# The first stage of a two-layer recurrent decoder step: order of its products, its sums of squares and one group's tables

## Chip, cores and metric

The kernel runs on one core of one Trainium2 chip. The metric is the device time of one execution in microseconds (us); the time before is the median of three runs.

## The reference, cut to what matters

One inference step of two layers over 1024 prompt tokens and 8 single new tokens, 1032 columns in all, model width 1024, float32. Each layer is

```
h = x * rsqrt(mean(x*x) + 1e-6) * norm_g
p = h @ w_in            # split over three groups of heads: HGRN2, GLA, S5
out = x + concat(group outputs, each gated) @ w_out
```

The third group (S5) takes two of the projections' tiles of 128 columns, called u here, and runs a diagonal complex recurrence over it. Its tables are powers of exp(A dt), so they need sines and cosines of small arrays (128 x 112). A last RMS norm follows the second layer.

## The kernel before, in words

Everything is held transposed: features on the 128 partitions, tokens along the free axis, cut into three blocks of 384, 384 and 264 columns (`BLK`). The width of 1024 is 8 slabs of 128 (`KD`). A float32 product is made of three products of rounded parts: weights and activations are each split into a high part (`wh`, `hh`) and a rest (`wl`, `lo`), and `wh*hh + wh*lo + wl*hh` is summed in PSUM over the 8 slabs (`gemm_tile`, L302). So one weight tile costs 24 products for each block. The norm's factor is applied last, when a finished sum leaves PSUM, so products can start before the norm is known.

Weights come through `WStream` (L252): halves of a tile are loaded (256 KB, two buffers), and each quarter is split by `do_split` (L274): ACT makes `wh`, then POOL or DVE makes `wl`. Six pairs of such quarters are held at a time; a tile takes four.

The first stage of layer 0 is written out by hand. `first_parts` (L220) issues the loads of x block by block with weight halves between them, and lets `parts` (L212) make `hh` on ACT and `lo` on DVE for each slab and block. Then two weight tiles (`UC0` and `UC0 + 1`, the third group's u) are multiplied (L714 to L719): the first for all blocks, the second block by block, and after each block `first_norm` (L236) squares x in place (ACT six of eight slabs, POOL two), adds the eight squares to two by six additions shared by DVE and POOL (L245), and sums these over the partitions by two products with a matrix of ones (`ones`, float32, not the rounded type). `rstd` (L200) turns the sum into the norm's factor `rn`: two operations on ACT, four on DVE. `ev_uc` (L700) multiplies the six finished sums by `rn` on DVE, which frees their six PSUM banks (two of the tag o, three of g, one of aux).

`masks()` (L1513) loads three masks; `prep(0)` starts `s5_prep` (L373), the third group's tables: some 36 small dependent DVE operations from L404 to L437, then powers by POOL (L362 to L367, tile `s5E` in `s5_thread`, L467). Both stand before the first stage's products in the text of layer 0.

The next work of TensorE in the text is a small projection `rbT` (PSUM tag o), then the projections of the second group (tag g). The order on each engine is not that of the text alone: a planner at build time lists the instructions of each engine by the order of the text and by when they become ready in its own model. Products that add to one PSUM bank keep the order of the text, and each engine's list is then fixed.

Of the kernel before, what the change touches and what calls it, by code (L numbers as in the profile page):

```python
# [38 lines left out]
def tile_hybrid_step(ctx: ExitStack, tc: tile.TileContext, a: dict, nl=NL, limit=RANGE):  # L39
# [160 lines left out]
    def rstd(pr, b):  # L200

        o, n = BLK[b]
        r = rn[:, o:o + n]
        t = tmp("sl", [P, 512], F32R).bitcast(F32)[:, :n]
        act(out=r, in_=pr, func=AF.Ln, scale=1.0 / 1024.0, bias=epsc)
        act(out=r, in_=r, func=AF.Exp, scale=-0.5)
        V.tensor_tensor(out=t, in0=r, in1=r, op=ALU.mult)
        V.scalar_tensor_tensor(out=t, in0=pr, scalar=1024.0 * EPS, in1=t, op0=ALU.add, op1=ALU.mult)
        V.tensor_scalar(out=t, in0=t, scalar1=-0.5 / 1024.0, scalar2=1.5, op0=ALU.mult, op1=ALU.add)
        V.tensor_tensor(out=r, in0=r, in1=t, op=ALU.mult)  # L210
# [9 lines left out]
    def first_parts(vec):  # L220
        xs = [alloc("x", [P, NT]) for _ in range(KD)]
        lo[:] = blocks(F32R)
        for b in range(3):
            o, n = BLK[b]
            for k in range(KD):
                if b == 0 and k % 4 == 0 or b and k == 0:
                    W.load(k // 4 if b == 0 else b + 1)
                SY.dma_start(out=xs[k][:, o:o + n], in_=a["xT"][:, k, o:o + n])
            for k in range(KD):
                if b == 0 and k % 2 == 0:  # L230
                    W.do_split(k // 2, V)
                parts(xs[k][:, o:o + n], k, b, vec)
        SY.dma_start(out=ident, in_=a["c_ident"])
        return xs

    def first_norm(xs, b):  # L236
        o, n = BLK[b]
        x = [t[:, o:o + n] for t in xs]
        for k in range(KD):
            if k % 4 == 3:  # L240
                G.tensor_tensor(out=x[k], in0=x[k], in1=x[k], op=ALU.mult)
            else:
                act(out=x[k], in_=x[k], func=AF.Square)
            if k > 1:
                (V if k % 2 else G).tensor_tensor(out=x[k % 2], in0=x[k % 2], in1=x[k], op=ALU.add)  # L245
        pr = psum("aux")
        for i in range(2):
            mm(pr[:, :n], ones, x[i], start=(i == 0), stop=(i == 1))
# [124 lines left out]
    def s5_prep(l, d):  # L373
# [30 lines left out]
        V.tensor_tensor(out=sn, in0=k14, in1=th.unsqueeze(1).to_broadcast([P, 14, 8]), op=ALU.mult)  # L404
# [255 lines left out]
    def layer(l, slow=False):  # L660
# [3 lines left out]
        wt = [W.push(a["wf"][l, i]) for i in range(25)]  # L664
# [21 lines left out]
        if l == 0:  # L686
            masks()
            prep(0)
# [22 lines left out]
        if l == 0:  # L711

            late = []
            gemm_tile(wt[UC0], [0, 1, 2], hrhs, lambda b, p: late.append(p), banks=("o", "o", "aux"))  # L714
            for b in range(3):
                gemm_tile(wt[UC0 + 1], [b], hrhs, lambda b, p: late.append(p), last=(b == 2))
                first_norm(xs, b)
                ev_uc(0)(b, late[b])
                ev_uc(1)(b, late[3 + b])  # L719
            for x in xs:  # L720
                release(x)
        else:
# [909 lines left out]
```

## Time and profile before

| | us |
|---|---|
| median of 3 runs (lowest to highest) | 1052.39 (1051.87 to 1053.72) |
| the profiled execution's own time | 1056.13 |
| its span, first to last instruction | 1054.2 |
| TensorE (PE) busy | 994.6 (94%) |
| VectorE (DVE) busy | 649.4 (62%) |
| ScalarE (ACT) busy | 479.2 (45%) |
| GpSimd (POOL) busy | 472.2 (45%) |

PE is the engine to look at: a gain elsewhere counts where it shortens a stretch in which PE waits or runs slowly. Matmuls overlap one another, so the time from the start of one to the start of the next is what one costs, not its duration.

### The profile page before, as it was taken

How to read it: one execution, taken by the hardware profiler on the slowest of the kernel's cores; microseconds unless marked ns; L12 is line 12 of the kernel's file. 1: busy time of each engine (PE TensorE's matmuls, PEld its weight loads, DVE VectorE, ACT ScalarE, POOL GpSimd, SP SyncE). 2: the span in 40 equal slices, each digit the busy share in tenths (PEclk: the TensorE clock that was granted, in tenths of full speed). 3: DMA queues.
4: the chain of work that ended last, by engine and by line, in shares of the span. 5: the costliest groups of instructions: out<-in, count | busy, mean ns of one | idle time of the engine just before them, and what ended most of it. 6: DMA issues, size and time to landing. Idle time of an engine off the chain costs nothing.

```text
span 1054.2 us, 20947 instructions
## 1 busy us (share of the span) xinstructions
PE 994.6 (94%) x8071; PEld 940.2 (89%) x8071; DVE 649.4 (62%) x1333; ACT 479.2 (45%) x995; POOL 472.2 (45%) x668
## 2 busy tenths in 40 slices
PE   6899999999999899999999999999999989999992
PEld 5788898899988799999999999888998988999991
DVE  8986745744767746685464682684388775553344
ACT  7334224554434656633332423445554475664431
POOL 4685754115355535542181476431344453552233
PEclk9999999899999989999999999999999998999996
DMA  7131131111111121144323114112111112112313
GB/s 245 46 107 51 42 107 46 59 50 56 54 40 38 57 73 60 48 137 136 128 78 92 48 41 113 45 47 61 41 56 53 41 53 70 54 48 88 116 51 135
DMA packets 78811, 76.77 MB, mean 73 GB/s; under 512 B 24524, under 2 KB 60652, under 8 KB 78700
## 3 DMA queue, kind: packets, MB, share of 16 engines
q1 hardware_dynamic: 78700, 75.33, 23.6%
q8 instruction: 65, 1.06, 0.4%
q14 instruction: 46, 0.38, 0.1%
HBM read 58.01 MB, written 15.53 MB: 70 GB/s over the span
## 4 chain that ended last, share of the span: by engine, by line
PE 68%; DVE 15%; POOL 7%; ACT 3%; issue 3%; DMA 2%; SPq 1%; DVEq 0%; POOLq 0%; ACTq 0%
PE ps_g L156 54%; PE ps_aux L156 8%; PE ps_o L156 5%; DVE s5W L584 1%; DVE Sp L897 1%; ACT ep L146 1%; DVE ep L873 1%; PE ps_aux L850 1%; POOL wl L289 1%; DVE onorm L1045 1%; DMA x<-in_xT 1%; ACT sg L146 1%; DVE wl L289 1%; DVE sl L907 1%; POOL s5E L364 1%
## 5 line engine op out<-in xcount | busy, mean ns | idle before, releaser
L156 PE MATMUL ps_g<-hh,wl 128*128 128x384 f32 (+1 forms) x1176 | 382.1, 326 | 4.5 <-POOL wl L289 4.5
L156 PE MATMUL ps_g<-hh,wh 128*128 128x384 f32 (+1 forms) x1176 | 384.6, 327 | 0.0
L156 PE MATMUL ps_g<-lo,wh 128*128 128x384 f32 (+1 forms) x1176 | 380.9, 324 | 0.0
L156 PEld LDWEIGHTS ps_g<-hh,wl 128*128 128x128 f32 x1176 | 223.5, 190 | 8.8 <-POOL wl L289 6.8
L156 PEld LDWEIGHTS ps_g<-hh,wh 128*128 128x128 f32 x1176 | 223.7, 190 | 5.3 <-issue 3.1
L156 PEld LDWEIGHTS ps_g<-lo,wh 128*128 128x128 f32 x1176 | 223.8, 190 | 1.0
L289 POOL TENSOR_TENSOR wl<-raw,wh 128x256 fp32r<-128x256 f32 x127 | 109.6, 865 | 219.9 <-ACT wh L146 207.0
L146 ACT ACTIVATE wh<-raw 128x256 fp32r<-128x256 f32 x258 | 102.2, 411 | 123.9 <-PE ps_g L156 111.5
L156 PE MATMUL ps_g<-m,wh 128*128 128x384 f32 (+1 forms) x567 | 135.7, 321 | 0.0
L289 DVE TENSOR_TENSOR wl<-raw,wh 128x256 fp32r<-128x256 f32 x131 | 82.1, 627 | 42.3 <-ACT wh L146 34.5
L156 PEld LDWEIGHTS ps_g<-m,wh 128*128 128x128 f32 x567 | 98.9, 188 | 0.5
L156 PE MATMUL ps_g<-m,wl 128*128 128x384 f32 (+1 forms) x261 | 82.9, 320 | 0.0
L1350 POOL TENSOR_TENSOR z<-z,sg 128x384 f32<-128x384 f32 (+1 forms) x48 | 47.3, 986 | 44.8 <-ACT sg L146 43.6
L156 PEld LDWEIGHTS ps_g<-m,wl 128*128 128x128 f32 x261 | 49.0, 188 | 0.1
L741 DVE TENSOR_TENSOR z<-ps_g,rn 128x384 f32<-128x384 f32 (+1 forms) x48 | 24.4, 509 | 32.8 <-PE ps_g L156 32.7
L146 ACT ACTIVATE sg<-z 128x384 f32<-128x384 f32 (+1 forms) x48 | 23.4, 487 | 28.9 <-DVE z L1348 28.7
L1360 DVE SCALAR_TENSOR_TENSOR onorm<-z,vec,onorm 128x384 f32<-128x384 f32 (+1 forms) x36 | 23.0, 639 | 21.3 <-POOL z L1350 21.2
L156 PE MATMUL ps_g<-vx,wh 128*128 128x384 f32 (+1 forms) x129 | 34.1, 322 | 0.0
L146 ACT ACTIVATE sg<-sg,ones 128x384 f32<-128x384 f32 (+2 forms) x52 | 32.3, 622 | 0.8
L146 ACT ACTIVATE sg<-sg 128x384 f32<-128x384 f32 (+2 forms) x56 | 31.8, 568 | 1.7 <-DVE sg L778 0.8
L156 PE MATMUL ps_o<-qs,Sp 64*64 64x64 f32 x360 | 23.4, 301 | 8.6 <-DVE Sp L897 8.6
L156 PEld LDWEIGHTS ps_o<-qs,Sp 64*64 64x64 f32 x360 | 21.2, 199 | 10.8 <-DVE Sp L897 9.6
(385 smaller groups left out, 1802.1 us busy)
## 6 DMA issues: line engine op xcount, KB each, us to landing
raw<-in_wf SPq DMA_DIRECT2D x100, 256.0 KB
raw<-in_wo SPq DMA_DIRECT2D x32, 256.0 KB
x<-in_xT SPq DMA_DIRECT2D x16, 192.0 KB
ext<-in_xT SPq DMA_DIRECT2D x16, 192.0 KB
x1d<-ext SPq DMA_DIRECT2D x16, 192.0 KB
ext<-x1d SPq DMA_DIRECT2D x16, 192.0 KB
usd<-ucp SPq DMA_DIRECT2D x4, 512.0 KB
s5U<-usd SPq DMA_DIRECT2D x32, 64.0 KB
```

What stands on the lines that cost most here:

```text
L146: return S.activation(out=out, in_=in_, func=func, **kw)
L156: return TE.matmul(out=out, lhsT=lhsT, rhs=rhs, start=start, stop=stop)
L289: e.tensor_tensor(out=wl, in0=r, in1=wh.bitcast(F32), op=ALU.subtract)
L364: e.tensor_tensor(out=dr, in0=dr, in1=t, op=ALU.subtract)
L584: V.tensor_tensor_scan(out=W_[:, ri, q], data0=m8[:, q0 + q:q0 + q + 1].to_broadcast([P, P]), data1=W_[:, ri, q], initial=0.0, op0=ALU.mul ...
L741: V.tensor_tensor(out=dst[:, o:o + n], in0=p, in1=rn[:, o:o + n], op=ALU.mult)
L850: TE.transpose(out=p[:, c * P:(c + 1) * P], in_=f[:, t0:t0 + P], identity=ident)
L873: V.tensor_tensor_scan(out=g[:, cs], data0=zero[:pr].to_broadcast([pr, ch]) if plus is None else plus[:, cs], data1=x[:, cs], initial=0.0, ...
L897: V.tensor_tensor_scan(out=s[:, :64 * n], data0=s[:, :64 * n], data1=kv[:, :64 * n], initial=0.0, op0=ALU.mult, op1=ALU.add)
L907: V.tensor_tensor(out=sl, in0=sq, in1=sh.bitcast(F32), op=ALU.subtract)
L1350: G.tensor_tensor(out=z[:, c], in0=z[:, c], in1=sg[:, c], op=ALU.mult)
L1360: V.scalar_tensor_tensor(out=on[:, c], in0=z[:, c], scalar=g, in1=on[:, c], op0=ALU.mult, op1=ALU.mult)
```

## The change

High parts first: for all three blocks and both tiles of u, the products with `hh` come first (`wh`, then `wl`), and the products with `lo` follow in a second pass; all six sums stay open in six PSUM banks. The second tile gets two slots of its own (`own`), so that both tiles are resident, and its loads and splits move up into the loading of x. The six additions of each block go, and eight products with ones replace two. The squares on ACT are held behind the last `hh` of the next block. `masks()` and `prep(0)` move behind the norm, and the sine and cosine chain's first operation (L404) is held behind the last `rn`. Splits made during loading alternate between DVE and POOL. `later` only orders two instructions of one engine's list.

```
@@ -207,7 +207,7 @@
         V.tensor_tensor(out=t, in0=r, in1=r, op=ALU.mult)
         V.scalar_tensor_tensor(out=t, in0=pr, scalar=1024.0 * EPS, in1=t, op0=ALU.add, op1=ALU.mult)
         V.tensor_scalar(out=t, in0=t, scalar1=-0.5 / 1024.0, scalar2=1.5, op0=ALU.mult, op1=ALU.add)
-        V.tensor_tensor(out=r, in0=r, in1=t, op=ALU.mult)
+        last["rn"] = V.tensor_tensor(out=r, in0=r, in1=t, op=ALU.mult)
 
     def parts(x, k, b, vec):
 
@@ -218,20 +218,33 @@
                                op0=ALU.mult, op1=ALU.subtract)
 
     def first_parts(vec):
+
         xs = [alloc("x", [P, NT]) for _ in range(KD)]
         lo[:] = blocks(F32R)
         for b in range(3):
             o, n = BLK[b]
             for k in range(KD):
-                if b == 0 and k % 4 == 0 or b and k == 0:
-                    W.load(k // 4 if b == 0 else b + 1)
+                if b < 2 and k % 4 == 0:
+                    W.load(2 * b + k // 4)
                 SY.dma_start(out=xs[k][:, o:o + n], in_=a["xT"][:, k, o:o + n])
             for k in range(KD):
-                if b == 0 and k % 2 == 0:
-                    W.do_split(k // 2, V)
-                parts(xs[k][:, o:o + n], k, b, vec)
+                if b < 2 and k % 2 == 0:
+                    W.do_split(4 * b + k // 2, G if k % 4 else V)
+                g = vec[:, V_NG + k:V_NG + k + 1]
+                x = xs[k][:, o:o + n]
+                h = hh[:, k, o:o + n]
+                last["hh", b] = act(out=h, in_=x, func=AF.Copy, scale=g)
+                last["lo", b] = V.scalar_tensor_tensor(out=lo[b][:, k, :], in0=x, scalar=g, in1=h.bitcast(F32), op0=ALU.mult,
+                                                       op1=ALU.subtract)
         SY.dma_start(out=ident, in_=a["c_ident"])
         return xs
+
+    last = {}
+
+    def later(i, other):
+
+        tc.add_manual_dep(getattr(i, "ins", i), getattr(other, "ins", other).name,
+                          mybir.DependencyInfo(mybir.DependencyClass.NoSync, mybir.DependencyReason.DATA), reason="order")
 
     def first_norm(xs, b):
         o, n = BLK[b]
@@ -240,12 +253,11 @@
             if k % 4 == 3:
                 G.tensor_tensor(out=x[k], in0=x[k], in1=x[k], op=ALU.mult)
             else:
-                act(out=x[k], in_=x[k], func=AF.Square)
-            if k > 1:
-                (V if k % 2 else G).tensor_tensor(out=x[k % 2], in0=x[k % 2], in1=x[k], op=ALU.add)
+                i = act(out=x[k], in_=x[k], func=AF.Square)
+                later(i, last["hh", min(b + 1, 2)])
         pr = psum("aux")
-        for i in range(2):
-            mm(pr[:, :n], ones, x[i], start=(i == 0), stop=(i == 1))
+        for k in range(KD):
+            mm(pr[:, :n], ones, x[k], start=(k == 0), stop=(k == KD - 1))
         rstd(pr[:, :n], b)
 
 
@@ -401,7 +413,9 @@
         V.tensor_tensor(out=th, in0=li, in1=dt, op=ALU.mult)
         G.tensor_tensor(out=lk, in0=k14[:, :8], in1=ld.unsqueeze(1).to_broadcast([P, 8, 8]), op=ALU.mult)
         act(out=mag, in_=lk, func=AF.Exp)
-        V.tensor_tensor(out=sn, in0=k14, in1=th.unsqueeze(1).to_broadcast([P, 14, 8]), op=ALU.mult)
+        i = V.tensor_tensor(out=sn, in0=k14, in1=th.unsqueeze(1).to_broadcast([P, 14, 8]), op=ALU.mult)
+        if l == 0:
+            later(i, last["rn"])
         V.tensor_scalar(out=n, in0=sn, scalar1=1.0 / (2 * PI), scalar2=MAGIC, op0=ALU.mult, op1=ALU.add)
         V.tensor_scalar(out=n, in0=n, scalar1=MAGIC, scalar2=None, op0=ALU.subtract)
         V.scalar_tensor_tensor(out=r, in0=n, scalar=-C1, in1=sn, op0=ALU.mult, op1=ALU.add)
@@ -661,7 +675,8 @@
         decodes[0] = 0
         vec = lv["vec"]
         col = lambda c: vec[:, c:c + 1]
-        wt = [W.push(a["wf"][l, i]) for i in range(25)]
+        own = [alloc("w1", [P, 2, 2, 2, P], F32R) for _ in range(2)] if l == 0 else []
+        wt = [W.push(a["wf"][l, i], [x[:, j] for x in own for j in range(2)] if own and i == 1 else None) for i in range(25)]
         if l == 0:
             with foreign():
                 pass
@@ -683,9 +698,6 @@
         vdd = dram.tile([8, 768], F32, name=nm("vdd"))
         st, onorm = {}, {}
 
-        if l == 0:
-            masks()
-            prep(0)
         wrr = tmp("kst", [P, 8, 16])
         SY.dma_start(out=wrr, in_=a["wr"][l])
         wr = tmp("Sp", [P, 1024], F32R)[:, :768].rearrange("p (k r c) -> p k r c", r=3, c=32)
@@ -710,15 +722,33 @@
 
         if l == 0:
 
-            late = []
-            gemm_tile(wt[UC0], [0, 1, 2], hrhs, lambda b, p: late.append(p), banks=("o", "o", "aux"))
+            late = [[psum("o"), psum("o"), psum("aux")], [psum("g") for _ in range(3)]]
+            W.do_split(9)
+            for part in range(2):
+                for b in range(3):
+                    o, n = BLK[b]
+                    for i in range(2):
+                        p = late[i][b][:, :n]
+                        ws = [W.get(wt[UC0 + i], k) for k in range(KD)]
+                        if part:
+                            for k, (wh, wl) in enumerate(ws):
+                                mm(p, wh, lo[b][:, k, :], start=False, stop=(k == KD - 1))
+                        else:
+                            for k, (wh, wl) in enumerate(ws):
+                                mm(p, wh, hh[:, k, o:o + n], start=(k == 0), stop=False)
+                            for k, (wh, wl) in enumerate(ws):
+                                mm(p, wl, hh[:, k, o:o + n], start=False, stop=False)
             for b in range(3):
-                gemm_tile(wt[UC0 + 1], [b], hrhs, lambda b, p: late.append(p), last=(b == 2))
                 first_norm(xs, b)
-                ev_uc(0)(b, late[b])
-                ev_uc(1)(b, late[3 + b])
+                for i in range(2):
+                    ev_uc(i)(b, late[i][b][:, :BLK[b][1]])
+            W.do_split(4 * wt[UC0 + 2] + 3)
+            for x in own:
+                release(x)
             for x in xs:
                 release(x)
+            masks()
+            prep(0)
         else:
             for i in range(2):
                 gemm_tile(wt[UC0 + i], [0, 1, 2], hrhs, ev_uc(i))
```

## Rows read from the trace of the kernel before

**Rows 1.** The page, part 1 (busy by engine) and part 4 (the chain by engine).
```profile
PE 994.6 (94%) x8071; PEld 940.2 (89%) x8071; DVE 649.4 (62%) x1333; ACT 479.2 (45%) x995; POOL 472.2 (45%) x668
...
PE 68%; DVE 15%; POOL 7%; ACT 3%; issue 3%; DMA 2%; SPq 1%; DVEq 0%; POOLq 0%; ACTq 0%
```

**Rows 2.** Busy us (and instructions) of each engine by stretch; then granted clock, DMA.
```profile
core 0: us, PE busy (x) PEld busy (x) DVE busy (x) ACT busy (x) POOL busy (x), PEclk, DMA share, GB/s
5.70:12.00 6.30, 5.22 (x14) 3.81 (x14) 5.36 (x16) 4.81 (x11) 1.51 (x2) 1.00 1.01 338
12.00:17.50 5.50, 3.75 (x12) 3.43 (x13) 5.50 (x12) 5.03 (x12) 3.67 (x4) 0.72 1.03 345
...
24.50:35.40 10.90, 8.90 (x51) 7.03 (x51) 10.79 (x25) 6.02 (x17) 5.18 (x7) 1.00 0.08 24
```

**Rows 3.** Timeline of PE in the first stage: start, duration, instruction, idle before and releaser.
```profile
5.71 0.69 PE L156 MATMUL ps_o<-hh,wh 128*128 128x384 f32 x1 [5.71 <-ACT hh L146]
...
14.49 0.69 PE L156 MATMUL ps_o<-lo,wh 128*128 128x384 f32 x1 [1.75 <-DVE lo L217]
...
17.54 0.48 PE L156 MATMUL ps_g<-hh,wh 128*128 128x384 f32 x1
...
22.06 0.34 PE L156 MATMUL ps_o<-lo,wh 128*128 128x384 f32 x1
...
23.11 0.34 PE L156 MATMUL ps_o<-lo,wh 128*128 128x384 f32 x1
...
30.20 0.28 PE L156 MATMUL ps_aux<-lo,wh 128*128 128x264 f32 x1
...
31.42 0.28 PE L156 MATMUL ps_g<-hh,wl 128*128 128x264 f32 x1
...
44.76 0.39 PE L156 MATMUL ps_o<-hh,Sp 128*96 128x384 f32 x1 [1.35 <-DVE s5p L430]
```

**Rows 4.** Timeline of PE: one product with ones, and the second product behind it.
```profile
39.09 0.81 PE L156 MATMUL ps_aux<-x,ones 128*128 128x384 f32 x2
...
39.91 0.34 PE L156 MATMUL ps_g<-hh,wh 128*128 128x384 f32 x1
```

**Rows 5.** Timeline of ACT while the first block of x arrives.
```profile
8.27 0.61 ACT L146 ACTIVATE hh<-x,vec 128x384 fp32r<-128x384 f32 x1 [0.97 <-DMA x<-in_xT]
...
9.20 0.70 ACT L146 ACTIVATE wh<-raw 128x256 fp32r<-128x256 f32 x2
...
11.15 1.61 ACT L146 ACTIVATE hh<-x,vec 128x384 fp32r<-128x384 f32 x3
```

**Rows 6.** Groups by line and shape, 0 to 60 us: busy, mean ns, idle before.
```profile
L217 DVE SCALAR_TENSOR_TENSOR lo<-x,vec,hh 128x384 fp32r<-128x384 f32 x16 | 11.9, 758 | 0.8 <-ACT hh L146 0.8
...
L245 POOL TENSOR_TENSOR x<-x,x 128x384 f32<-128x384 f32 x6 | 7.6, 1271 | 0.9 <-ACT x L146 0.9
```

**Rows 7.** Timelines of DVE and POOL: the tables' last steps, the powers' first and last.
```profile
46.09 0.26 DVE L433 TENSOR_TENSOR s5p<-s5p 128x112 f32<-128x112 f32 x1
...
46.23 0.41 POOL L438 COPY pv<-s5p 128x56 f32<-128x56 f32 x2 [0.92 <-DVE s5p L432]
...
70.28 0.73 POOL L367 TENSOR_TENSOR s5E<-s5E,s5Bm 128x256 f32<-128x256 f32 x1
```

**Rows 8.** Groups of the third group's output `yc`: durations min/median/max, first and last start.
```profile
L1358 DVE TENSOR_TENSOR yc<-z,yc x6: 421/546/558, 392.5 to 409.8; 128x384 f32<-128x384 f32 x4, 128x264 f32<-128x264 f32 x2
...
L785 POOL TENSOR_TENSOR yc<-yc,sg x2: 2415/2421/2427, 236.8 to 246.7; 128x1032 f32<-128x1032 f32 x2
```

**Rows 9.** Timelines of PE and DVE around the third group's product with `t`.
```profile
82.21 0.39 PE L156 MATMUL ps_aux<-ud,t 128*128 128x8 f32 x2 [1.76 <-DVE bm L879]
...
86.22 0.33 PE L156 MATMUL ps_g<-hh,wh 128*128 128x384 f32 x1
...
91.30 0.56 DVE L741 TENSOR_TENSOR vf<-ps_g,rn 128x384 f32<-128x384 f32 x1 [4.76 <-PE ps_g L156]
```

**Rows 10.** Busy us by stretch, the end of layer 0's recurrences; columns as in rows 2.
```profile
300.00:372.00 72.00, 61.99 (x740) 58.03 (x740) 49.40 (x86) 38.68 (x81) 37.02 (x40) 0.91 0.16 48
```

**Rows 11.** Waits of PE, 100 to 140 us: total us, times, longest.
```profile
PE ps_g L156 <- POOL wl L289: 1.3, 1, 1.3
```

## The prediction

> **What bounds the kernel now.** I read the page first: PE is busy 94% of the span and carries 68% of the chain that ended last [rows 1]. So the question for any edit is what it adds to PE's work and what it takes from the time in which PE waits or runs slowly. Then the stretches of the first stage: DVE is busy without a gap from 12.0 to 17.5 us and for 10.79 of the 10.90 us up to 35.4, while PE is busy only 3.75 of 5.50 us in the one and 8.90 of 10.90 in the other [rows 2]. Then PE's own timeline, for what it waits for (`lo` from DVE, as at 14.49) and at what pace it runs [rows 3]. The first stage does lose PE time, and to DVE.
>
> **How much it loses.** From the first product (5.71) to the first product behind the stage (44.76) pass 39.05 us [rows 3]. The work in it: two tiles, three blocks, 24 products each, so 96 products of 384 columns and 48 of 264. Unhindered, they cost 0.175 us (six from 22.06 to 23.11) and 0.122 us (ten from 30.20 to 31.42) [rows 3]: 96 x 0.175 + 48 x 0.122 = 22.66 us. To this come six products with ones. From 39.09 to 39.91 PE does one of them and one plain product [rows 4], so it costs 0.82 - 0.175 = 0.645 us, 3.7 times a plain one; for 264 columns 0.645 x 264/384 = 0.443. Four and two of these are 3.47 us. Lost are 39.05 - 22.66 - 3.47 = 12.92 us. That is all the stage can give back.
>
> **The change part by part.**
>
> Products with ones: eight for two in each block, so 18 more, 12 x 0.645 + 6 x 0.443 = +10.40 us of PE. Could they hide in PE's waits? The waits lie early, before the squares exist: the change holds block 0's squares behind block 1's last `hh`, and x, loaded at 338 to 345 GB/s to the end of the stretch at 17.5 [rows 2], sets when that is. I count them in full.
>
> What is still lost afterwards. (a) In one bank products keep their order, so PE first needs all eight `hh` of block 0 with `wh`, and cannot fill in `lo` and `wl` products as before. ACT has slab 3 at 8.27; slab 4 half a microsecond later, a pair of weight splits (0.70), slabs 5 to 7 (1.61) [rows 5]; without the squares that lay between them the eighth is there at about 8.27 + 0.5 + 0.5 + 0.7 + 1.61 = 11.6. PE will have done 8 x 0.175 = 1.4 us of work in 5.9: 4.5 lost. (b) From then on work is plentiful (the `wl` products of block 0, the second tile, block 1), and PE should be dense. But it enters this stretch after a sparse one. After its waits before 14.49 PE made nine products in 3.05 us (to 17.54), 1.48 us more than at full pace [rows 3], in a stretch whose granted clock is 0.72 [rows 2], that is partly at 1.2 instead of 2.4 GHz. I take 1.5 lost here too. Bounds for (b): nothing, if the clock is up by 11.6, to 1.5 plus the 2.0 us that PE idles between 24.5 and 35.4 [rows 2], if the fixed order meets late `lo` again. I take 1.5, since the entry is like that at 14.49 and DVE is relieved (below).
> On this clock the Trainium skill speaks against the change (TensorE: Matmul & The Clock Gate, Part 1: The HAM clock gate): the throttled state is the default and activity releases it. The slow products after 14.49 agree with it. By it the thin start leaves the array slow, and the sum is the one below; the granted clock of 1.00 that the row writes for 5.7 to 12.0 [rows 2], taken at its word, would make it 1.5 us less.
>
> The sum for the stage: +10.40 - 12.92 + 4.5 + 1.5 = **+3.5 us**, between +2.0 and +5.5.
>
> DVE and POOL additions: 18 go. POOL's took 1.27 us each, and `lo` beside them takes 758 ns on average [rows 6]. This is what lets `lo` come in time; its worth is already in the waits counted as gone, so it has no term of its own.
>
> Loads, splits, slots: no product or byte is added. The second tile's second half (256 KB) moves from before block 2 into the middle of block 1, whose last four slabs come 0.8 us later at 345 GB/s [rows 2], while PE is still behind with block 0. Cost nothing; were PE not behind, 0.8 us. On SP the masks' loads stand behind the norm, with each later one waiting for the cast before; queued behind them are weight halves of tiles needed only after `rbT`. Nothing, bounded by the 2.0 us of idle time above.
>
> Masks and tables: the chain of about 36 DVE operations may not start until the last `rn`, which needs PE's last product with ones, at about 44.8 + 3.5 = 48.3. Each follows the one before by some 0.2 us (0.26 long at the end of the chain [rows 7]): over 7 us, plus some 2.5 for the norm's own operations. The tables come at about 58 instead of 46.3, and the powers on POOL (46.23 to 71.0 [rows 7]) some 12 us later. Who waits? The third group's output is made by 249 us and first used at 392.5 [rows 8], 143 us of cover. So the delay itself costs nothing; what it does is to meet other work elsewhere, which the rivals price.
>
> The span would be 1054.2 + 3.5 = 1057.7. That execution took 1056.13 us itself, 3.7 above the median of the runs shown; I add the difference to the median: 1052.4 + 3.5 = **1055.9**. About 0.2% (2.1 us) can be told from no change.
>
> **The rivals.**
>
> Not slower: the wait at 82.21. PE stands 1.76 us before the third group's product with `t`, because the copy that makes `t` is queued on DVE behind the second group's scans, and PE then runs slowly until 86.22 [rows 9]. At the pace of nine products in 3.05 us, 48% of those 4.0 us are lost, 1.9; in all 3.7. With the third group 12 us later, that copy falls at about 93, where DVE waits for PE (4.76 us idle before 91.30 [rows 9]). Then 3.5 - 3.7 = -0.2: 1052.2. For it: the place is plain. Against it: PE's list is fixed at build time, and a product placed too early stalls as well at 93 as at 82. It decides once 1.4 of the 3.7 us are gone.
>
> Faster: the above, and less waiting at the end of layer 0, where PE is busy only 61.99 of 72 us [rows 10]. There the recurrences of the first group hold PE up. If the second group's get DVE and POOL before the third group's, the chain starts earlier relative to PE. A quarter of the 10 us: -0.2 - 2.5 = -2.7, so 1049.7. Against it: that chain starts from products which come 3.5 us later.
>
> Slower still: POOL. Its powers, now 12 us later, come between weight splits that PE needs; one wait of this kind is there already, 1.3 us [rows 11]. Three more: +3.9, so 1059.8.
>
> The change doing less than it says is possible in one way only: the planner may still put early `lo` products between high ones of other banks. That moves none of the terms, since PE is dense there.
>
> **How the numbers follow.** The forecast (+2.0 to +5.5, 1054.4 to 1057.9) gets 0.37: its terms are counts times measured spacings, and only the 6.0 of new losses is estimated. POOL 0.10. Not slower 0.27, as its place is clear but the list is fixed. Faster 0.26: two gains together, but each wait downstream is re-planned, and I can't exclude that more of them go than come. So slower 0.47, same 0.27, faster 0.26. The range, 1049.0 to 1060.0, leaves out about half of the faster case and a little of the POOL case, under 2 in 10.
>
> **What would show it.** In the profile after: 24 products with ones, each in two records, 0.645 us for 384 columns; the first eight products spread to about 11.6; a dense PE from there to about 48; `rn` of the last block near 51; the tables at about 58. I am wrong if PE is past the stage before 44.8 us, which needs less than 2.5 us lost in it, or if the wait at 82 is gone with nothing in its place.

## The result and the profile after

The kernel after takes 1058.84 us (median of five runs, 1057.22 to 1061.42), the kernel before 1052.39 in the same comparison: a ratio of 1.0061, with a 95% interval of 1.0043 to 1.0078, so 4.5 to 8.2 us slower. The forecast was 1055.9 in a range of 1049.0 to 1060.0. Sign and range were right. Where the time went was only half right, as the profile shows.

The profiled execution took 1058.75 us, its span is 1056.9. Of the kernel before a second execution was profiled later (the first experiment below: span 1050.3), and both are used here, because the one shown ahead of the prediction was itself 3.7 us above its median.

The page of the kernel after, parts 1 and 4, answers to [rows 1]:

```profile
PE 1002.7 (95%) x8107; PEld 947.6 (90%) x8107; DVE 653.9 (62%) x1322; ACT 477.8 (45%) x995; POOL 459.9 (44%) x661
...
PE 69%; DVE 15%; POOL 8%; ACT 4%; issue 2%; DMA 1%; SPq 0%; DVEq 0%; POOLq 0%; ACTq 0%
```

PE is busy 8.1 us more than in the execution shown ahead of the prediction, and 10.2 more than in the second (992.5); it still sets the span. So the time has to be looked for in PE's work and in PE's waits.

Busy time by stretch, columns as in [rows 2]; the first three rows answer to [rows 2], the fourth to [rows 10], the last is new and serves as a measure for every kernel below:

```profile
5.70:12.00 6.30, 4.99 (x10) 3.10 (x11) 5.61 (x11) 5.51 (x13) 2.11 (x4) 1.00 1.02 349
12.00:17.50 5.50, 5.50 (x30) 5.50 (x30) 5.50 (x9) 5.47 (x13) 3.65 (x4) 1.00 1.08 369
24.50:35.40 10.90, 10.90 (x72) 10.10 (x71) 3.95 (x12) 4.26 (x13) 3.02 (x5) 1.00 0.19 59
300.00:372.00 72.00, 68.07 (x775) 64.64 (x772) 53.23 (x107) 38.03 (x78) 40.83 (x43) 0.95 0.17 50
...
50.00:300.00 250.00, 237.59 (x1928) 218.90 (x1928) 160.78 (x341) 97.36 (x182) 119.00 (x188) 0.97 0.20 60
```

In the first stage the products run dense: from 12.0 to 17.5 us PE is busy for the whole stretch at a granted clock of 1.00 (3.75 of 5.50 us and 0.72 before), from 24.5 to 35.4 it never stops, and DVE has fallen from 10.79 to 3.95 us. DVE no longer holds PE up there. But from 50 to 300 us PE now stands idle for 250 - 237.59 = 12.41 us; in the second execution of the kernel before it is 6.19:

```profile
50.00:300.00 250.00, 243.81 (x2055) 223.97 (x2053) 154.48 (x328) 101.41 (x190) 126.48 (x183) 0.99 0.21 62
```

The timeline of PE, which answers to [rows 3, 4, 9]:

```profile
5.74 1.19 PE L156 MATMUL ps_o<-hh,wh 128*128 128x384 f32 x2 [5.74 <-ACT hh L146]
7.28 1.20 PE L156 MATMUL ps_o<-hh,wh 128*128 128x384 f32 x2 [0.34 <-ACT hh L146]
9.39 2.20 PE L156 MATMUL ps_o<-hh,wh 128*128 128x384 f32 x4 [0.92 <-ACT hh L146]
11.40 2.32 PE L156 MATMUL ps_o<-hh,wl 128*128 128x384 f32 x8
13.55 1.39 PE L156 MATMUL ps_o<-lo,wh 128*128 128x384 f32 x7
...
33.37 14.04 PE L156 MATMUL ps_aux<-x,ones 128*128 128x384 f32 x48
47.05 0.53 PE L156 MATMUL ps_o<-hh,Sp 128*96 128x384 f32 x1
...
97.84 0.45 PE L156 MATMUL ps_g<-hh,wl 128*128 128x384 f32 x1 [2.45 <-POOL wl L301]
...
105.45 0.28 PE L156 MATMUL ps_aux<-ud,t 128*128 128x8 f32 x2
```

The stage can be read off in these rows. Eight thin products until 11.40; then the products stand 0.320 us apart until 13.0 and 0.175 from 13.2 on, full pace; the 24 products with ones (48 records) in one block from 33.37; the next stage at 47.05, that is 2.3 us later than the 44.76 of [rows 3] and 3.05 later than the 44.00 of the second execution. The product with `t` no longer waits (1.76 us of wait in [rows 9]), but it has another place: 105.45 instead of 82.21. The planner has listed PE's work anew. And at 97.84 PE waits 2.45 us for a weight split from POOL, which it did not before.

DVE's timeline has the held chain, which answers to [rows 7]:

```profile
50.31 0.27 DVE L416 TENSOR_TENSOR s5p<-s5q,sm 128x112 f32<-128x112 f32 x1
50.49 0.55 DVE L839 TENSOR_TENSOR sq<-ps_o,rn 96x384 f32<-96x384 f32 x1
...
62.68 0.62 DVE L851 TENSOR_SCALAR sB<-ps_o,vec 128x384 f32<-128x384 f32 x1
63.22 0.27 DVE L442 TENSOR_TENSOR s5p<-s5p 128x112 f32<-128x112 f32 x1
...
65.52 0.55 DVE L451 TENSOR_TENSOR pw<-s5q,s5p 128x64 f32<-128x64 f32 x2
```

And POOL's the end of the tables and of the powers:

```profile
65.77 0.81 POOL L452 COPY pv<-s5p 128x56 f32<-128x56 f32 x2
...
96.38 0.72 POOL L376 TENSOR_TENSOR s5E<-s5E,s5Bm 128x256 f32<-128x256 f32 x1
97.06 0.72 POOL L301 TENSOR_TENSOR wl<-raw,wh 128x256 fp32r<-128x256 f32 x1
...
99.00 0.73 POOL L379 TENSOR_TENSOR s5E<-s5E,s5Bm 128x256 f32<-128x256 f32 x1
```

The chain starts right behind the last `rn`, at 50.31, but takes until 65.77. Its steps are 0.2 to 0.3 us long; between them DVE does the scalings of the next stage (`sq`, `sB`, `vf`), at 0.5 us and more each. So the tables come 19.5 us later than in [rows 7], not 12, and the powers end at 99.7 instead of 71.0. At 97.06 a weight split stands among them, the one PE waits for at 97.84.

The waits of PE from 75 to 300 us, which answer to [rows 11] (total us, times, longest):

```profile
PE ps_g L156 <- POOL wl L301: 3.3, 2, 2.4
PE ps_aux L1174 <- ACT s5Bm L146: 2.8, 1, 2.8
...
PE ps_aux L156 <- POOL s5O L620: 1.4, 1, 1.4
```

`s5Bm` and `s5O` are tiles of the third group. The wait for `s5Bm` is a chain of three engines: ACT's copy out of a PSUM bank into `s5Bm` waits for POOL's powers, and PE (163.15) waits for that bank with transposes of the second group. ACT's row:

```profile
162.50 0.60 ACT L146 ACTIVATE s5Bm<-ps_aux 128x512 f32<-128x512 f32 x1 [7.03 <-POOL s5E L379]
```

And the group's output, which answers to [rows 8]:

```profile
L1388 DVE TENSOR_TENSOR yc<-z,yc x6: 423/546/558, 399.5 to 416.8; 128x384 f32<-128x384 f32 x4, 128x264 f32<-128x264 f32 x2
...
L815 POOL TENSOR_TENSOR yc<-yc,sg x2: 2409/2416/2422, 254.1 to 263.9; 128x1032 f32<-128x1032 f32 x2
```

It is made at 254 to 266 and used at 399.5: 133 us of cover are left. The output was never late, and still the time was lost before it. At its first use the kernel is 10.5 us behind the second execution of the kernel before (399.5 against 389.0): 3.05 by the stage's end, 7.4 between. The span is only 6.6 longer, so 3.9 of them come back later, and no run shows where from.

### The profile page after: what moved, and what is told of

Its sections match the earlier page's. It is cut to its first block, busy times and chain, and to the rows that moved or that the text cites. A ratio compares the mean times of both kernels' runs of the same rounds, so it can differ in the third digit from the quotient of the medians.

```text
span 1056.9 us, 21006 instructions
## 1 busy us (share of the span) xinstructions
PE 1002.7 (95%) x8107; PEld 947.6 (90%) x8107; DVE 653.9 (62%) x1322; ACT 477.8 (45%) x995; POOL 459.9 (44%) x661
## 4 chain that ended last, share of the span: by engine, by line
PE 69%; DVE 15%; POOL 8%; ACT 4%; issue 2%; DMA 1%; SPq 0%; DVEq 0%; POOLq 0%; ACTq 0%
PE ps_g L156 52%; PE ps_aux L156 9%; PE ps_o L156 6%; DVE ep L903 2%; DVE s5W L598 2%; DVE Sp L927 1%; ACT ep L146 1%; DVE onorm L1075 1%; POOL s5E L376 1%; PE ps_aux L880 1%; POOL wl L301 1%; DVE qbd L954 1%; DVE wl L301 1%; POOL s5Bm L375 1%; POOL s5E L377 1%
## 5 line engine op out<-in xcount | busy, mean ns | idle before, releaser
L156 PE MATMUL ps_g<-hh,wl 128*128 128x384 f32 (+1 forms) x1152 | 374.7, 326 | 6.9 <-POOL wl L301 5.8
L156 PE MATMUL ps_g<-hh,wh 128*128 128x384 f32 (+1 forms) x1152 | 375.3, 326 | 0.0
L156 PE MATMUL ps_g<-lo,wh 128*128 128x384 f32 (+1 forms) x1152 | 373.2, 324 | 0.0
L156 PEld LDWEIGHTS ps_g<-hh,wl 128*128 128x128 f32 x1152 | 219.1, 190 | 11.9 <-POOL wl L301 7.8
L156 PEld LDWEIGHTS ps_g<-hh,wh 128*128 128x128 f32 x1152 | 219.0, 190 | 4.0 <-issue 2.0
L156 PEld LDWEIGHTS ps_g<-lo,wh 128*128 128x128 f32 x1152 | 218.6, 190 | 1.6 <-issue 0.6
L301 POOL TENSOR_TENSOR wl<-raw,wh 128x256 fp32r<-128x256 f32 x127 | 105.5, 833 | 246.5 <-ACT wh L146 226.2
L937 DVE TENSOR_TENSOR sl<-sq,sh 128x512 fp32r<-128x512 f32 x24 | 20.5, 853 | 15.3 <-ACT sh L146 15.3
```

The costliest lines, as they stand in the source:

```text
L156: return TE.matmul(out=out, lhsT=lhsT, rhs=rhs, start=start, stop=stop)
L301: e.tensor_tensor(out=wl, in0=r, in1=wh.bitcast(F32), op=ALU.subtract)
L937: V.tensor_tensor(out=sl, in0=sq, in1=sh.bitcast(F32), op=ALU.subtract)
```

## The experiments

Each kernel's ratio is to the kernel before, run beside it. "Stage's end" is the start of the first product with `Sp` on PE, "tables" the start of the copy to `pv` on POOL, "idle" is 250 us less PE's busy time between 50 and 300 us, "clock" the granted clock of that stretch, "first use" the start of the first `yc<-z,yc`, with its distance from the stage's end behind it. All but the ratio come from one profiled execution each.

| kernel | ratio, 95% interval | stage's end | tables | idle, clock | first use, distance |
|---|---|---|---|---|---|
| before, second execution | 1 | 44.00 | 45.47 | 6.19, 0.99 | 389.0, 345.0 |
| after | 1.0061, 1.0043 to 1.0078 | 47.05 | 65.77 | 12.41, 0.97 | 399.5, 352.5 |
| e1 | 0.9986, 0.9971 to 1.0002 | 47.77 | 32.23 | 4.83, 0.99 | 391.2, 343.4 |
| e2 | 1.0014, 1.0000 to 1.0028 | 42.87 | 65.74 | 8.74, 0.97 | 391.7, 348.8 |
| e3 | 0.9981, 0.9961 to 1.0002 | 47.81 | 41.77 | 5.31, 0.98 | 390.0, 342.2 |
| f1 | 1.0031, 1.0009 to 1.0052 | 40.61 | 57.50 | 14.17, 0.97 | 401.0, 360.4 |
| f2 | 1.0113, 1.0088 to 1.0138 | 41.50 | 60.72 | 10.27, 0.97 | 399.5, 358.0 |
| f3 | 1.0078, 1.0055 to 1.0101 | 48.86 | 67.58 | 6.78, 0.95 | 402.9, 354.0 |
| f4 | 1.0114, 1.0084 to 1.0145 | 48.07 | 59.00 | 9.49, 0.96 | 405.5, 357.4 |
| g1 | 0.9996, 0.9980 to 1.0013 | 42.94 | 32.66 | 7.23, 0.99 | 384.4, 341.5 |
| g2 | 0.9956, 0.9939 to 0.9973 | 43.01 | 32.63 | 4.48, 0.98 | 386.6, 343.6 |
| g3 | 0.9917, 0.9896 to 0.9939 | 41.31 | 32.19 | 6.45, 0.98 | 383.3, 342.0 |
| g4 | 0.9913, 0.9888 to 0.9937 | 39.87 | 32.67 | 6.06, 0.98 | 384.8, 344.9 |

The last column is the finding. Seven kernels whose tables are ready by 45.5 us need 341.5 to 345.0 us from the stage's end to the third group's first use; the six whose tables come at 57.5 or later need 348.8 to 360.4. (The execution shown ahead of the prediction, the one 3.7 us above its median, has 392.5 - 44.76 = 347.7, between the two.) How far one execution can be trusted, g1 and g2 show: their instructions are the same, in the same order on each engine, up to 800 us, and yet the first use is at 384.4 and 386.6 and the idle time 7.23 and 4.48.

The column does not say which of two things costs. Every edit makes the planner list PE's work anew, and the lists go with the tables. Between 50 and 390 us the seven kernels have nearly the same order of PE's products, the six have others: the first product with `t` stands 32.0 to 37.5 us behind the stage's end in the seven (81.25 in e1) and 46.5 to 59.5 in the six (105.45 in the kernel after). No run has late tables in the old list, or early ones in the new. So where "late" is said to cost below, it is the lateness together with the list that the planner makes for it.

**e0: the kernel before again.**

> The kernel before, once more, for a second trace of it: the one shown took 1056.13 us, 3.7 above its own median. Every theory expects about 1052.4 us (span about 1050.5); the 3.7 us should be found in one or two places of the first trace (its end, or waits in layer 0), and the first stage should again hand over to the next work at 44.5 to 45 us.

1052.14 us, span 1050.3. PE in the second execution:

```profile
44.00 0.39 PE L156 MATMUL ps_o<-hh,Sp 128*96 128x384 f32 x1 [1.35 <-DVE s5p L430]
```

The stage ends with the same wait of 1.35 us as in [rows 3]; most of the 3.7 us of the first execution lay elsewhere: 0.8 were lost by here and 3.5 by the first use of `yc` (392.5 against 389.0). Note what PE waits for: a step of the tables. In the kernel before they were in the way of the stage's own end.

**e1: the tables not held.** Everything else of the change stays.

```
-        i = V.tensor_tensor(out=sn, in0=k14, ...)
-        if l == 0:
-            later(i, last["rn"])
+        V.tensor_tensor(out=sn, in0=k14, ...)
```

> The changed kernel, but the sine and cosine chain is not held behind the last norm factor; DVE may do it in its idle time during the first stage. Theory T (the stage itself costs 2.3 us, the other 4 come from the third group's work meeting weight splits and the second group some 12 us later): 3 to 5 us faster than the changed kernel, 1053.8 to 1055.8. Rival R (the delay is free under its cover of 143 us, and the products with ones cost it all): within 1.5 us of 1058.8.

1052.5 us, ratio 0.9986: 0.75% less than the kernel after, 7.9 us by the ratios (6.3 by the medians, which are from two comparisons). The stage ends no earlier (47.77). Its tables on POOL, its waits of PE from 75 to 300, and its stretch from 50 to 300:

```profile
32.23 0.41 POOL L450 COPY pv<-s5p 128x56 f32<-128x56 f32 x2 [1.61 <-DVE s5p L444]
```

```profile
PE ps_aux L878 <- DVE atts L1209: 1.4, 1, 1.4
PE ps_aux L156 <- POOL s5O L618: 0.6, 1, 0.6
```

```profile
50.00:300.00 250.00, 245.17 (x2078) 227.04 (x2076) 158.22 (x324) 101.16 (x190) 120.12 (x169) 0.99 0.21 62
```

The tables end at 32.2, in time that the removed additions leave free on DVE and POOL, and the long waits for `wl`, `s5Bm` and `s5O` are gone. So the hold is the costly part of the change, and without it the 3.8 us of the stage are made up for. The theory of the late third group held; its size was put too low.

**e2: the additions back, tables held; e3: the additions back, tables not held.**

```
-        for k in range(KD):
-            mm(pr[:, :n], ones, x[k], start=(k == 0), stop=(k == KD - 1))
+            if k > 1:
+                (V if k % 2 else G).tensor_tensor(out=x[k % 2], in0=x[k % 2], in1=x[k], op=ALU.add)
+        for i in range(2):
+            mm(pr[:, :n], ones, x[i], start=(i == 0), stop=(i == 1))
```

> The changed kernel with the six additions and two products with ones per block as before; high parts first and the held tables stay. 18 products with ones fewer are 10.4 us of PE. R: 1058.8 - 10.4 plus up to 2 for waits on the additions, 1048.4 to 1050.4. T: the last norm factor, and so the tables, come some 10 us earlier too, so part of the 4 goes as well: 1044.5 to 1049. Rival D (the additions were what made PE wait for lo, through DVE and POOL): PE waits again in the first stage, 1052 or more.

> Both edits: additions back and tables not held, so high parts first is what stays of the change, with the masks and tables behind the norm in the text. T: 1044 to 1048, no more than 2 us faster than with the additions alone. R: as with the additions alone within 1.5. D: 1052 or more, since tables and additions are both back on DVE.

1055.04 us (1.0014) and 1051.64 us (0.9981). Against the kernel after, e2 gains half a per cent; against e1, e3 gains nothing. Between e2 and e3 the hold costs 0.33%, some 3.4 us (their intervals touch), less than half of what it costs with eight products, though the tables come as late in e2 (65.74) as in the kernel after. PE in e2 and in e3, the third block's products with ones:

```profile
41.04 2.10 PE L156 MATMUL ps_aux<-x,ones 128*128 128x264 f32 x4 [3.66 <-DVE sl L208]
```

```profile
45.88 2.10 PE L156 MATMUL ps_aux<-x,ones 128*128 128x264 f32 x4 [5.28 <-POOL s5U L493]
```

18 products with ones fewer, some 10 us of PE, bring the stage's end forward by 4.2 us in e2 and not at all in e3 (47.81 against 47.77). Where PE worked, it now waits. The ranges of T and R failed in both runs (for e3, T's was 1044 to 1048). D's bound of 1052 is passed in e2 and missed by 0.4 in e3; its mechanism, additions and tables in DVE's way, is in e3's trace: PE also waits 2.82 us at 39.69 for an addition on DVE. The release that the profile names at 45.88 is a fill of 0.15 us on POOL, hardly the cause. What e2 names, the step that reads the first block's sum, ends just ahead of it in e3 too, and is followed up below:

```profile
45.18 0.56 DVE L208 SCALAR_TENSOR_TENSOR sl<-ps_aux,sl 128x384 f32<-128x384 f32 x1
```

**f1: sums of squares in the rounded type.** The squares lose their low bits in this kernel and in all g.

```
-    ones = cst.tile([P, P], F32, name="ones")
+    onesr = cst.tile([P, P], F32R, name="ones")
...
-            mm(pr[:, :n], ones, x[k], start=(k == 0), stop=(k == KD - 1))
+            mm(pr[:, :n], onesr, sq[k][:, o:o + n], start=(k == 0), stop=(k == KD - 1))
...
+            sq = [alloc("sq", [P, NT], F32R) for _ in range(4)]
+            first_squares(xs, sq, range(4))
...
```

> The kernel after with the tables not held (as in the run before it that moved them), and the sums of squares made by products of a type of one pass: the squares are written rounded into free slots (those of k 4 to 7 into the slots that x 0 to 3 leave), and the ones are of the rounded type too. The squares lose low bits by this. Theory 1 (the ones' price on PE is what the stage still loses): a float32 product of 384 columns took 0.645 us, one of rounded type 0.175, so the 24 products fall from 14.0 us to about 3.8; PE leaves the stage at 37 to 40 instead of 47.8, and half of the 10 us or more survives: ratio to the kernel before 0.988 to 0.995, 1041 to 1048 us. Theory 2 (what the products with ones cost is only a cover for something else, as the run with the additions back showed: there PE waited where it had worked): PE waits for squares, for the norm or for weights at 38 to 48, and the time is within 2 us of the same kernel with float32 ones, ratio 0.997 to 1.001.

1055.23 us, ratio 1.0031. The stage ends at 40.61, 7.2 us earlier than in e1, and yet the kernel is slower than e1. (Its profiled execution took 1061.24, 6 us above its median, so its row in the table is on the high side.) POOL shows why:

```profile
39.25 0.56 POOL L415 MEMSET s5q<- 128x8 f32 x14 [3.84 <-PE ps_aux L156]
...
57.50 0.46 POOL L455 COPY pv<-s5p 128x56 f32<-128x56 f32 x2 [15.92 <-DVE s5p L449]
```

The tables' tile `s5q` took a slot that the squares had filled; it had to wait until PE had read them, at 39.25. The edit had made the tables late by itself, without a hold. Neither theory was tested; g1 mends it.

**f2: the kernel before, with the tables alone moved behind the norm and held.**

```
-        if l == 0:
-            masks()
-            prep(0)
...
             for x in xs:
                 release(x)
+            masks()
+            prep(0)
```

(and the hold, as in the change)

> The kernel before, with one part of the change alone: masks and the third group's tables are written behind the norm, and the chain of the sines is held until the last block's norm is ready. Products, sums of squares and weights stay as before. Theory 1 (late tables are what costs, in whatever kernel): the tables end at 60 to 66 instead of 46, PE waits for POOL's and DVE's pieces of the third group between 90 and 300, and the time is 3 to 8 us above the kernel before, ratio 1.003 to 1.008; the stage itself hands over at 43 to 45 as before. Theory 2 (the tables collide only with what the changed weight loads and their splits put there): no more than 1.5 us slower, ratio under 1.0015.

1064.09 us, ratio 1.0113: 9.3 to 14.5 us slower, by this one part of the change, although the stage ends 2.5 us earlier (41.50). That is theory 1, at more than its price. Late tables cost with the old first stage and the old weight loads too, so they do not collide with the new weight loads in particular. (Behind the stage f2 has a new list as well: its first product with `t` is at 99.72.)

**f3: the powers on DVE.**

```
-                cmul(G, E_[:, 0, :, m:2 * m], ...)
+                cmul(G if l else V, E_[:, 0, :, m:2 * m], ...)
```

> The kernel after with one chain of the third group of the first layer, the repeated multiplications that make the powers, on DVE instead of POOL; everything stays as late as it is. Theory 1 (the late group costs because its chain shares POOL with the weight splits, which is the mechanism of the rival named slower still): the waits of PE for wl from POOL near 98 (2.45 us) and for the s5 tiles from POOL go, and the time falls by 2.5 to 6 us, to 1053 to 1056, ratio 1.000 to 1.004. Theory 2 (it costs because the group as a whole comes late, on whichever engine): the waits change their engine, DVE for POOL, and the time stays within 2 us of the kernel after or rises, ratio 1.004 to 1.009.

1060.91 us, ratio 1.0078, no better than the kernel after. PE's waits from 75 to 300:

```profile
PE ps_aux L156 <- DVE s5O L623: 2.5, 1, 2.5
PE ps_aux L156 <- POOL s5O L620: 1.6, 1, 1.6
```

The waits for `wl` from POOL are gone, and `s5O` from DVE has taken their place; PE's waits are shorter in all (idle 6.78), but its granted clock from 50 to 300 is 0.95, so a larger part of its work was done at 1.2 instead of 2.4 GHz: 27.3 us, where the clock records of the traces show 13.9 in the kernel after and 6.8 in the second execution of the kernel before. The time is in theory 2's range: it is the late group that costs, on whichever engine.

**f4: held to the first block's norm instead of the last.**

```
-        last["rn"] = V.tensor_tensor(...)
+        last["rn", b] = V.tensor_tensor(...)
...
-            later(i, last["rn"])
+            later(i, last["rn", 0])
```

> The kernel after with the sines' chain held until the norm of the first block instead of that of the last. The tables should end some 10 us earlier, near 54 to 57 instead of 65.8 (not held: 32). Theory 1 (the price grows with the delay): the time lies between the two, 1053.5 to 1057, ratio 1.001 to 1.0045. Theory 2 (one collision, there or not): it is either that of the kernel after (ratio over 1.0045) or that of the kernel without the hold (ratio under 1.000).

1065.3 us, ratio 1.0114: worse than the kernel after, although the chain starts 7.3 us earlier (42.97) and ends 6.8 earlier (59.00). The first theory, that the price grows with the delay, fell. Of the second only this is left: by 57.5 us every kernel pays. Why this one pays as much as f2 stays open; its list is neither the old one nor that of the kernel after (first product with `t` at 94.58).

**g1: rounded squares, with two slots kept for the tables.**

```
+            hold = [alloc("s5", [P, NT]) for _ in range(2)]
+            sq = []
+            for k in range(0, KD, 2):
+                sq += [alloc("sq", [P, NT], F32R) for _ in range(2)]
+                first_squares(xs, sq, (k, k + 1))
...
```

> As the run with rounded squares, with one thing mended: there the tables' tiles took the slots that the squares had filled, so that the sines began only behind the products with ones (41.5 us) and the tables ended at 57.5, late again without any hold. Here two free slots are kept for the tables, and the squares go two at a time into slots that x has left. The squares lose low bits as there. Theory 1 (the third group costs by how long after the stage's end its tables are ready): tables at 31 to 36 with the stage ending at 40 to 42, so the price of the late group is gone and the 7 us that the shorter products save on PE stay in part: 1043 to 1050 us, ratio 0.990 to 0.997. Theory 2 (the time is set by other collisions that any shift of the stage brings): the gain of the stage is lost again between 75 and 400 us, ratio 0.999 to 1.005.

1052.78 us, ratio 0.9996. Tables at 32.66, first use at 384.4, 4.6 us ahead of the kernel before: theory 1 so far. But the end of the span, 1051.0, has nothing of it. PE and POOL in the second layer:

```profile
806.90 0.69 PE L156 MATMUL ps_g<-hh,wl 128*128 128x384 f32 x1 [4.13 <-POOL wl L306]
```

```profile
804.75 0.61 POOL L976 TENSOR_TENSOR dV<-dV,k 128x256 f32<-128x256 f32 x1 [3.97 <-DMA dV<-vdd]
805.44 0.73 POOL L977 TENSOR_TENSOR dS<-dS,dV 128x256 f32<-128x256 f32 x1
806.12 1.41 POOL L306 TENSOR_TENSOR wl<-raw,wh 128x256 fp32r<-128x256 f32 x2
```

Two weight splits stand in POOL's queue behind a step that waits 3.97 us for a DMA. The Trainium skill says of such a queue that ACT, DVE and POOL take their instructions strictly first in, first out (TensorE: Matmul & The Clock Gate, the table at its head). The trace agrees: POOL sat idle for 3.97 us with the splits behind, though ACT had made the `wh` that they need by 800.0.

**g2: these two splits on DVE.**

```
-                e = eng or (V if self.split % 2 else G)
+                e = eng or (V if self.split % 2 or self.split in (198, 200) else G)
```

> The run before this one (rounded squares, tables early) was 4.6 us ahead of the kernel before from 440 to 780 us and lost it between 780 and 830, in the second layer, where PE waited 4.13 us at 806.90 for two weight splits that stood on POOL behind multiplications of the second half's vdd, which wait for a DMA. Here these two splits (198 and 200 of the stream) go to DVE, which sat idle from 803 to 810. Theory 1 (the loss is this one place in POOL's queue): the 4 us stay, 1046 to 1050 us, ratio 0.993 to 0.997. Theory 2 (another wait takes its place in the second layer, as in the stage itself): ratio 0.998 to 1.002.

1047.82 us, ratio 0.9956. Theory 1: the wait at that place is gone, and two instructions on another engine brought back 4.2 us by the ratios. (The lead of 4.6 us was that of one execution; g2's at the first use is 2.4.)

**g3: the first block's norm ahead of the last `lo` products.** With it the squares move ahead of all `lo` products.

```
+                    if part and b == 2:
+                        first_norm(sq, 0)
...
-                first_norm(sq, b)
+                if b:
+                    first_norm(sq, b)
```

> The run before this one still had one wait of PE at the stage's end: 3.71 us at 41.08, ahead of the third block's products with ones, released by the step of the first block's norm that reads its sum (DVE, at 40.48). All three banks with the name aux are in use by then (the last block of the first tile, and the sums of the first two blocks), so that the third sum has to wait until the first is read; and on DVE that read stood behind a step of the third group's tables which waited for POOL. Here the first block's products with ones are written before the last block's products with lo. Theory 1 (PE waits for the bank): the wait falls to under 1 us, PE leaves the stage at 39 to 41 instead of 43.0, and 1 to 4 us of it stay: ratio 0.991 to 0.996. Theory 2 (the stage's end is set by the norm and what follows on DVE, not by the bank): another wait takes its place at the first product with Sp or behind it, and the ratio stays at 0.9945 to 0.9985.

1043.91 us, ratio 0.9917. The wait that g2 had for the bank is gone:

```profile
41.08 1.31 PE L156 MATMUL ps_aux<-sq,ones 128*128 128x264 f32 x8 [3.71 <-DVE sl L209]
```

A wait with the same releaser stands in e2 (3.66 us) and g1 (4.27); in the kernel after 14 us of products with ones lie over that place. The stage ends 1.7 us earlier (41.31), not 2 to 4, for another wait took part of its place, on PE and, for its cause, on DVE:

```profile
41.31 0.60 PE L156 MATMUL ps_o<-hh,Sp 128*96 128x384 f32 x1 [3.51 <-DVE ucp L720]
```

```profile
39.06 0.69 DVE L380 TENSOR_TENSOR t<-pw,bb 128x512 f32<-128x512 f32 x1 [2.16 <-POOL bb L384]
```

So each theory has a part: the bank was the wait, and the norm on DVE is the next.

**g4: one step of the tables held behind the norm.** The multiplication at 39.06, and the one before it.

```
+        if after is not None:
+            later(x, after)
+            later(y, after)
...
+                 last["rn"] if l == 0 and hf == 0 else None)
```

> The run before this one lost its wait for the bank, but PE then stood 3.51 us at 41.31 before the first product with Sp, released by the scaling of the first block (ucp, DVE): between two steps of the first block's norm DVE had a multiplication of the tables with bb (its second, 39.06) in its queue, which waited 2.16 us for POOL. Here that step and the one before it are held until the last block's norm is ready, as the change holds the sines, but at the end of the chain instead of its start. Theory 1 (a step held costs only what needs it soon; the next user of these products is PE at about 75 to 80): the wait at 41 falls by 2.5 to 3.5 us and stays gone, ratio 0.987 to 0.991. Theory 2 (any hold of the third group pays again downstream, as the change's own did): ratio 0.9915 or more.

1042.92 us, ratio 0.9913, between the ranges of the two theories. PE at the stage's end, and its largest new waits between 300 and 420:

```profile
39.87 0.39 PE L156 MATMUL ps_o<-hh,Sp 128*96 128x384 f32 x1 [0.77 <-DVE ucp L724]
```

```profile
PE ps_aux L998 <- ACT dV L146: 3.7, 2, 3.1
```

The wait fell from 3.51 to 0.77 us, as theory 1 had it, and PE's idle time from 50 to 300 did not grow. The ratio is nevertheless that of g3: the first use of `yc` comes at 384.8 against 383.3, and two waits for `dV`, 3.7 us in all, lie between 300 and 420, where g3 has none (it has one of 1.5 before 300). No cost of this hold shows between 50 and 300 us; in these two executions what it gains is given back at the end of the layer. That the hold is the reason is not shown. g3 and g4 are the fastest kernels of the study, 0.8 to 0.9% below the kernel before, with squares that are rounded.

## Why the prediction was right, and where it was wrong

**The stage: right.** From 5.74 to 47.05 are 41.31 us. Products with ones: 13.68 from their first to the next product, where 3.47 + 10.40 = 13.87 were forecast. Still lost: 41.31 - 22.66 - 13.68 = 4.97, where 6.0 were forecast. Of term (a), 4.5, came 4.26 (5.66 us until 11.40, less 1.40 of work). Of term (b), 1.5, came 0.75: eight products in 2.15 us, then full pace. That is one execution's value, and no error of the forecast: from the ninth product to full pace, the same products in the same order lose 1.5 us in f4, 1.8 in e2 and 2.1 in f3, so 1.5 lies in the middle, and the stage's end moves with it (48.07 in f4, 48.86 in f3). In all of them the products stand 0.320 us apart at first and 0.175 later. On this the clock's rule in the Trainium skill (TensorE: Matmul & The Clock Gate, Part 1: The HAM clock gate), that the throttled state is the default and activity releases it, agrees with the trace in its sign. The granted clock of 1.00 that the rows write for 5.7 to 12.0 us contradicts it only in appearance: the first clock record of the trace begins at 13.06, where the pace rises, and ahead of it there is none. The sum: +2.3 us against the shown execution, +3.05 against the second, where +3.5 was forecast.

**"So the delay itself costs nothing": wrong.** This is the step that failed. The hold costs 7.9 us in the changed kernel (e1 against after) and 3.4 with the additions back (e3 against e2); with the move in the text it costs 11.9 in the kernel before (f2). The argument looked at the group's last product, `yc`, and at its 143 us of cover [rows 8]. That cover is real, 133 us of it are left, but it covers only the last step. The steps between meet PE in three ways that the trace shows: the powers stand on POOL around a weight split that PE waits 2.45 us for (97.84); the copy to `s5Bm`, behind the powers, keeps a bank from the second group's transposes for 2.82 us (163.15); and `s5O` is an input of products on PE (1.4 us). Besides, the argument kept PE's list as it was, only later; the planner wrote another one. How the price divides between late steps and new list is not shown. Two of the prediction's own rows could have told: the wait at 82.21 for the copy that makes `t` [rows 9], and the wait for a split on POOL [rows 11].

**The tables at 58: wrong, 65.8.** About 36 steps at 0.2 us were counted as if DVE had nothing else to do. Behind the norm it has the scalings of the stage and of the next: 15.5 us from 50.31 to 65.77.

**The rival "slower still": the mechanism was there, its engine was not the point.** Two waits for `wl`, 3.3 us in all where three of 1.3 were priced, and further ones for `s5Bm` and `s5O`. f3 took the powers off POOL and gained nothing. The rival's 1059.8 is nearer to the 1058.84 measured than the forecast is.

**The rivals "not slower" and "faster": gains came, and were not enough.** "Not slower" put the copy that makes `t` at about 93 and held PE's list against it as fixed. In the kernel after the product with `t` stands at 105.45 and waits for nothing; in e1 it stands at 81.25 and waits for nothing either. But in its place PE waits at 97.84, and then runs at 1.2 GHz from 98.4 to 101.8. From 300 to 372 PE is busy 68.07 us instead of 61.99 [rows 10], though this stretch is not quite the same work, as it comes later; moved by the 10.5 us of the first use (310.5 to 382.5) it is 65.72. So it was partly luck that the forecast's 1055.9 was not far off: of the cost that it put at nothing, 7.4 us by the first use, 3.9 came back behind it, which no term had.

**Waiting or clock.** Both, in shares that differ from run to run. Against the second execution of the kernel before, PE idles 6.2 us more between 50 and 300 us in the kernel after and spends 7.1 us more at 1.2 GHz, of which some 45% is lost (0.320 against 0.175 us for a product): an estimate of 3.2 us. In f3 it is 0.6 us of waiting and 20.5 more at 1.2 GHz, some 9.3 lost.

**Not settled:** why the tables at 59.0 (f4) cost more than those at 65.8; whether late steps or the list that the planner makes for them cost the time; and where the 3.9 us come back.

## What to carry to other kernels

Cover has to be counted for each step of a chain, at the engine and the queue where it will stand, not from the chain's last product to its first use. If work off the critical path must give way to the critical one, hold the one step that is in the way rather than the start of its chain: held at the start, the whole chain met the next stage's work and cost 3.4 to 7.9 us, while the one step (g4) took 2.7 us from a wait and left the time where it was. An edit of this kind also changes the planner's lists, so look where PE's products stand afterwards before a wait is put down to the delay. And when work is taken off the bounding engine and nothing comes of it, look for the wait that the work had covered: here a PSUM bank, and then a step of the norm.

## What was not expected of the hardware

A float32 product of 384 columns costs 3.7 times a rounded one, 0.645 against 0.175 us: the profile has it as two records 0.322 us apart. In f1 sixteen rounded products with ones take 2.97 us. The Trainium skill (FP8 and Floating Point Precision, TensorE Precision Notes) has a true float32 product as four passes through the array; the factor of 3.7 comes close to it. It was not expected that taking these passes away would be worth nothing by itself: in g1 the stage ended 4.8 us earlier than in e1 at a ratio that can't be told from e1's, until the waits that came out behind it had been removed one by one.
